# RWKV blocks of a hybrid encoder layer: one layout for both halves of the partitions, and the state's own part as small products in the chain

## The chip, the core and the metric

The kernel runs on one core of a Trainium2 chip (trn2). Its engines are TensorE (PE, matrix products, with its weight loads shown apart as PEld), VectorE (DVE), ScalarE (ACT), GpSimd (POOL) and SyncE (SP), which here issues nearly all DMA transfers. The metric is the time on the device in microseconds (us) of one execution, lower is better; the profile is of one execution.

## What is computed

One encoder layer over 2048 tokens of width 1024: a norm, one input projection, four token mixers side by side (retention, RWKV-7, a gated linear recurrence "LRU", gated linear attention "GLA", 256 columns and 4 heads of 64 each), an output projection, and 16 experts that each choose 256 tokens. The change lies in the RWKV-7 mixer, which runs a matrix state over time, once forward and once backward:

```python
def _rwkv7_direction(r, k, v, xw, xa, ...):
    ...
    def step(S, inp):
        r_t, w_t, k_t, v_t, kk_t, a_t = inp
        sa = jnp.einsum('bhvk,bhk->bhv', S, -kk_t)
        S = (S * w_t[:, :, None, :] + sa[..., None] * (kk_t * a_t)[:, :, None, :]
             + v_t[..., None] * k_t[:, :, None, :])
        return S, jnp.einsum('bhvk,bhk->bhv', S, r_t)
    ...
    _, y = lax.scan(step, jnp.zeros((B, N_GROUP_HEADS, HEAD_DIM, HEAD_DIM), r.dtype), xs)

def _rwkv7_group(...):
    y_f, b_f = _rwkv7_direction(r, k, v, ...)
    y_b, b_b = _rwkv7_direction(_flip(r), _flip(k), _flip(v), ...)
    y = y_f + _flip(y_b)
```

All inputs and outputs are fp32.

## The kernel before

The program goes through the stages projection with LRU and the RWKV inputs (`rwkv_a`), then RWKV blocks with retention and GLA beside them, then the output projection, a top-k, and the experts. In the middle stage three generators are woven (`weave`): `rwkv_rest` (the RWKV blocks, then the output weights and four early tiles of the output projection), `retention` and `gla`, in fixed shares of steps. That gives the order in which the work is written; a scheduler of the framework then places each engine's instructions, so the order on an engine differs from the written one. Each engine works through its own list in order.

RWKV works on chunks of 64 tokens, two chunks to a block of 128, 16 blocks a direction. `rwkv_b` runs rounds: in round i it prepares block i of both directions (`rwkv_prep`), runs the chain of the blocks prepared a round before (`rwkv_chain`), and loads the next blocks (`rwkv_load`); `in_turn` takes one step of each in turn. Partition halves 0 to 63 and 64 to 127 are called H[0] and H[1]; a chunk of index e uses them in an order that depends on e.

`rwkv_load` brings the block's row `bld` (640 KB), four pieces into `q1` and two into `ti`, the inverse that was computed earlier. `rwkv_prep` then makes, for four heads: p1, transposed keys (L606), which ACT moves to `q0` and `q1` with four instructions of 64 partitions (L610); p2, transposed z and v (L615), moved to `R` and `mv` (L618, L619); two banks of 64-row products (L628), masked into `R` by four DVE instructions (L633); products of keys with `rd`, a layout with zero halves that DVE copies from `bld` (L623), on PE at L639 and masked into `q0` and `q1` by four DVE instructions (L643); X = ti x R (L648), evacuated by ACT (L650); and E = q1 - X x q0 (L656, L659), a 128x128 matrix per head and chunk. `q0`, `q1` and `rd` are rings of fixed tiles, zeroed once in the halves that nothing writes; `q1` holds two identity blocks as well (`eye`).

`rwkv_chain` takes the two chunks in turn. Per chunk: four products of `E` with `mv`, one per head (L672), into one bank. One half of that bank is the new state, which DVE scales by the chunk's decay into the next chunk's `mv` (L676); the other is the output, which ACT copies to `yt` (L680), stored by SP (L683).

A bank is 512 fp32 values on each partition; the RWKV stream has four. A product in fp32 is two records in the profile, each with a weight load of its own. `tile_position` places a product on part of PE's 128x128 array.

## Time and profile before

| what | value |
|---|---|
| median of 3 runs | 2882.82 us (2876.65 to 2886.56) |
| the profiled execution, its own time | 2875.32 us |
| its span, first to last instruction | 2873.5 us |
| busy: PE / PEld / DVE / ACT / POOL | 2597.0 / 2323.1 / 1762.4 / 1381.8 / 724.3 us |
| mean granted PE clock | 0.944 of full speed |

A busy time is the time in which an instruction of that engine was running, summed without overlap. Matmuls are pipelined: a record of PE lasts longer than the distance to the next one, so the distance between starts tells the rate. "Idle before" is the time in which the engine stood just before the group's instructions, and behind the arrow stands what ended it. The granted clock is the share of full speed that the chip gave PE.

### The profile page before, as it was taken

The page shows a single profiled execution, that of the slowest core. Times are in us where ns is not written, and L with a number is a line of the kernel's source. Part 1 is how long each engine was busy: PE and PEld are TensorE (multiplying, and loading weights), DVE is VectorE, ACT ScalarE, POOL GpSimd, SP SyncE. Part 2 cuts the span into 40 slices and gives each one's busy share as a digit, 9 for nine tenths or more (in the row PEclk, how much of TensorE's full clock was granted, in tenths as well). Part 3 has the DMA queues.
Part 4 walks back from the last instruction along what each step waited for, and adds up shares of the span by engine and source line. Part 5 has one row for each costly group of instructions (what it writes and reads, how often), then busy time and mean ns, then how long its engine had stood idle before and what let it go on. Part 6 is the DMA issues. An engine that isn't in the chain of part 4 may idle for free.

```text
span 2873.5 us, 47388 instructions
## 1 busy us (share of the span) xinstructions
PE 2597.0 (90%) x18433; PEld 2323.1 (81%) x18433; DVE 1762.4 (61%) x3458; ACT 1381.8 (48%) x2302; POOL 724.3 (25%) x764
## 2 busy tenths in 40 slices
PE   6989998989878888896979659999999999999987
PEld 5866787778767777774767549999999999999987
DVE  4444567767787667888444465555555555566564
ACT  4265555435434666554533214444444444455453
POOL 0011115444524554446533310000000000000121
PEclk9999999989989989897989869999999999999999
DMA  9735554775546544445344436666666666798874
GB/s 316 268 112 184 169 167 150 215 230 167 137 115 176 171 143 147 142 135 177 109 164 142 150 97 206 206 206 206 206 206 206 206 206 206 221 294 294 264 238 142
DMA packets 474016, 538.41 MB, mean 187 GB/s; under 512 B 129952, under 2 KB 411584, under 8 KB 473024
## 3 DMA queue, kind: packets, MB, share of 16 engines
q1 hardware_dynamic: 461984, 492.12, 53.0%
q0 software_dynamic: 11808, 43.26, 5.7%
q8 instruction: 145, 2.38, 0.3%
q14 instruction: 79, 0.65, 0.1%
HBM read 392.17 MB, written 145.23 MB: 187 GB/s over the span
## 4 chain that ended last, share of the span: by engine, by line
PE 57%; DVE 14%; DMA 8%; ACT 6%; issue 4%; POOL 3%; SPq 0%; POOLq 0%; ACTq 0%; DVEq 0%
PE bank L129 46%; DMA ld<-rw_cm 3%; DMA rt_ld<-tm 1%; PE bank L639 1%; PE bank L1486 1%; DVE x L485 1%; PE bank L656 1%; DMA fn_x<-acc,x_idx 1%; PE bank L628 1%; DVE pr L484 1%; PE bank L672 1%; DVE tk_j L1389 1%; POOL pr L484 1%; PE bank L648 1%; PE bank L1467 1%
## 5 line engine op out<-in xcount | busy, mean ns | idle before, releaser
L44 DVE TENSOR_TENSOR x_wl<-x_st,x_wh 128x2048 fp32r<-128x2048 f32 x189 | 432.9, 2292 | 304.1 <-ACT x_wh L43 303.7
L129 PE MATMUL bank<-x_xh,x_wh 128*128 128x256 f32 x2048 | 580.4, 285 | 2.7 <-ACT x_wh L43 2.6
L129 PE MATMUL bank<-x_xl,x_wh 128*128 128x256 f32 x2048 | 577.8, 283 | 0.0
L129 PE MATMUL bank<-x_xh,x_wl 128*128 128x256 f32 x2048 | 572.6, 283 | 1.1 <-DVE x_wl L44 1.1
L43 ACT ACTIVATE x_wh<-x_st 128x2048 fp32r<-128x2048 f32 x192 | 367.6, 1915 | 119.6 <-PE bank L129 100.4
L129 PEld LDWEIGHTS bank<-x_xh,x_wh 128*128 128x128 f32 x2048 | 393.7, 192 | 3.5 <-ACT x_wh L43 3.0
L129 PEld LDWEIGHTS bank<-x_xl,x_wh 128*128 128x128 f32 x2048 | 393.6, 192 | 0.0
L129 PEld LDWEIGHTS bank<-x_xh,x_wl 128*128 128x128 f32 x2048 | 390.4, 192 | 1.6 <-DVE x_wl L44 1.6
L129 PE MATMUL bank<-x_wh,x_hh 128*128 128x256 f32 x1024 | 289.9, 285 | 5.7 <-ACT x_hh L43 5.7
L129 PE MATMUL bank<-x_wl,x_hh 128*128 128x256 f32 x1024 | 291.1, 285 | 0.0
L129 PE MATMUL bank<-x_wh,x_hl 128*128 128x256 f32 x1024 | 289.6, 284 | 0.0
L1612 POOL DMA_INDIRECT acc<-x_os,x_idx x30 | 48.6, 1620 | 925.3 <-ACT x_os L1546 896.7
L129 PE MATMUL bank<-h_hi,w_hi 128*128 128x512 f32 x576 | 238.3, 417 | 20.8 <-DVE o_cm L1662 13.3
L129 PE MATMUL bank<-h_lo,w_hi 128*128 128x512 f32 x576 | 239.7, 416 | 0.0
L129 PE MATMUL bank<-h_hi,w_lo 128*128 128x512 f32 x576 | 235.9, 410 | 0.0
L129 PEld LDWEIGHTS bank<-x_wh,x_hh 128*128 128x128 f32 x1024 | 196.5, 193 | 5.9 <-ACT x_hh L43 5.9
L129 PEld LDWEIGHTS bank<-x_wl,x_hh 128*128 128x128 f32 x1024 | 197.3, 193 | 0.0
L129 PEld LDWEIGHTS bank<-x_wh,x_hl 128*128 128x128 f32 x1024 | 197.1, 193 | 0.0
L129 PE MATMUL bank<-w_hi,h_hi 128*128 128x256 f32 (+1 forms) x512 | 156.5, 306 | 12.9 <-DVE o_tm L1662 9.4
L129 PEld LDWEIGHTS bank<-h_hi,w_hi 128*128 128x128 f32 x576 | 112.2, 195 | 56.8 <-DVE o_cm L1662 15.9
L129 PE MATMUL bank<-w_lo,h_hi 128*128 128x256 f32 (+1 forms) x512 | 149.0, 291 | 0.0
L129 PE MATMUL bank<-w_hi,h_lo 128*128 128x256 f32 (+1 forms) x512 | 148.4, 290 | 0.0
(448 smaller groups left out, 5520.9 us busy)
## 6 DMA issues: line engine op xcount, KB each, us to landing
x_st<-in_exp_w_gate_dram SPq DMA_DIRECT2D x64, 1024.0 KB, 8.7
x_st<-in_exp_w_up_dram SPq DMA_DIRECT2D x64, 1024.0 KB, 9.2
x_st<-in_exp_w_down_dram SPq DMA_DIRECT2D x64, 1024.0 KB, 5.3
w_st<-in_w_in_dram SPq DMA_DIRECT2D x20, 1024.0 KB, 7.6
rw_sp<-sp SPq DMA_DIRECT2D x16, 1280.0 KB, 4.6
bld<-rw_sp SPq DMA_DIRECT2D x32, 640.0 KB, 3.9
ld<-rw_cm SPq DMA_DIRECT2D x14, 899.5 KB, 6.2
cm<-o_cm SPq DMA_DIRECT2D x40, 256.0 KB, 2.8
```

Source lines behind the costliest of these rows:

```text
L43: g.nc.scalar.activation(out=hi, in_=src, func=AF.Copy)
L44: (g.nc.gpsimd if pool else g.nc.vector).tensor_tensor(out=lo, in0=src, in1=hi.bitcast(F32), op=OP.subtract)
L129: g.nc.tensor.matmul(out, lhsT=lhs[a][:, k, lsl], rhs=rhs[b][:, k, rsl], start=(k + i == 0 and out is outs[0]), stop=(3 * k + i == 3 * nk ...
L484: eng.tensor_tensor(out=pr[:, 0:i, 0:i], in0=a, in1=b, op=OP.mult)
L485: nc.vector.tensor_reduce(out=x[:, 0:i, i], in_=pr[:, 0:i, 0:i], axis=AX.X, op=OP.add)
L628: nc.tensor.matmul(pss[k][:, q * P:(q + 1) * P], lhsT=z[q][H[k]], rhs=ks, start=True, stop=True)
L639: nc.tensor.matmul(ps[:, o:o + P], lhsT=bk[q][e], rhs=rd[:, 2 * q + 1 - e], start=True, stop=True)
L648: nc.tensor.matmul(ps[:, h * P:(h + 1) * P], lhsT=ti[:, h], rhs=R[:, h], start=True, stop=True)
L656: nc.tensor.matmul(ps[:, h * 256:(h + 1) * 256], lhsT=X[:, 2 * h2 + h, :], rhs=q0[:, 2 * h2 + h].rearrange("p e c -> p (e c)"), start=True ...
L672: nc.tensor.matmul(ps[:, h, :], lhsT=E[:, h, e, :], rhs=mv[e][:, h, :], start=True, stop=True)
L1389: nc.vector.tensor_scalar(out=junk, in0=vals, scalar1=cand[:, m:m + 1], scalar2=0.0, op0=OP.is_ge, op1=OP.add, accum_out=cnt[:, m:m + 1])
L1612: g.nc.gpsimd.indirect_dma_start(out=dst, out_offset=bass.IndirectOffsetOnAxis(ap=idx[:, s:s + 1], axis=0), in_=t[:, s], in_offset=None, **kw)
```

## The change

`q0` and `q1` become one tile `Q`, [chunk, head, 128 columns], with the same layout on both partition halves: its first 64 columns come from p1 by one ACT instruction, its last 64 from the masked products by one DVE instruction. `R` is laid out alike: one ACT instruction, and two DVE ones where there were four. `rd` is no longer copied by DVE but loaded by two DMAs a block. In L628's place, 8 products of 64x64 per block on the four quarters of the array replace 4 of 64x128. `E` is built without the part that multiplies the state directly: 16 products of 64x64 weights on 128 columns replace 4 of 128x128 on 256, into two banks, one per chunk; a mask column `hm` picks the half of `Q` that is added. The part left out moves to the chain: per chunk, one product with a 64x64 identity over 256 columns and four with `rq` (the transposed keys, loaded by the four DMAs that filled `q1`, now issued in the prep) accumulate in the bank before 8 products with `E` of 128x64 weights.

```diff
@@ rwkv_b_buffers
-    g.rd = ring("rd", [P, 4, 2, C], 2, lambda t: [t[64 * k:64 * k + 64, :, 1 - k, :] for k in range(2)])
-    g.q0 = ring("q0", [P, NH, 2, P], 2, lambda t: [t[64 * e:64 * e + 64, :, 1 - e, :] for e in range(2)])
-    g.q1 = ring("q1", [P, NH, 2, P], 4, eye)
+    g.rd = ring("rd", [P, 4, 2, C], 4, lambda t: [t[64 * k:64 * k + 64, :, 1 - k, :] for k in range(2)])
...
+    g.hm = g.fp.tile([P, 2], F32, name="hm")
+    nc.vector.memset(g.hm, 1.0)
+    for e in range(2):
+        nc.vector.memset(g.hm[64 * e:64 * e + 64, e:e + 1], 0.0)
@@ rwkv_load
-    q1 = turn(g.q1)
-    for k in range(2):
-        for e in range(2):
-            s = slice(64 * e, 64 * e + 64)
-            nc.sync.dma_start(out=q1[s, k::2, e, s], in_=half[64 * k:64 * k + 64, :, 320 - 320 * e:384 - 320 * e])
...
+    rd = turn(g.rd)
+    for k in range(2):
+        s = slice(64 * k, 64 * k + 64)
+        nc.sync.dma_start(out=rd[s, :, k], in_=sp[s].rearrange("p (u t) -> p u t", t=320)[:, :, 0:C])
@@ rwkv_prep
+    Q = g.bp.tile([P, 2, NH, P], F32, name="Q", tag="Q")
...
+    rq = g.mp.tile([P, NH, C], F32, name="rq", tag="rq")
...
+    for k in range(2):
+        for e in range(2):
+            nc.sync.dma_start(out=rq[H[e], k::2], in_=half[H[k], :, 320 - 320 * e:384 - 320 * e])
...
-    for e in range(2):
-        for s, q in ((H[e], q0), (H[1 - e], q1)):
-            nc.scalar.activation(out=qh(q[s, :, e, H[1 - e]]), in_=p1[s, :, e], func=AF.Copy)
+    nc.scalar.activation(out=Q[:, :, :, 0:C], in_=p1.rearrange("p (e h c) -> p e h c", e=2, h=NH), func=AF.Copy)
...
+    nc.scalar.activation(out=R[:, :, 0:C], in_=p2[:, 0], func=AF.Copy)
     for e in range(2):
-        nc.scalar.activation(out=R[H[e], :, H[e]], in_=p2[H[e], 0], func=AF.Copy)
         nc.scalar.activation(out=mv[e][H[1 - e]], in_=p2[H[1 - e], 1], func=AF.Copy)
...
-    rd = turn(g.rd)
-    for k in range(2):
-        nc.vector.tensor_copy(out=rd[H[k], :, k], in_=ld[H[k]].rearrange("p (u t) -> p u t", t=320)[:, :, 0:C])
...
-            nc.tensor.matmul(pss[k][:, q * P:(q + 1) * P], lhsT=z[q][H[k]], rhs=ks, start=True, stop=True)
+            for e in range(2):
+                o = HALF * q + C + 3 * C * (1 - e)
+                nc.tensor.matmul(pss[k][H[e], q * C:(q + 1) * C], lhsT=z[q][H[k], H[e]], rhs=ld[H[k], o:o + C], start=True, stop=True,
+                                 tile_position=(64 * k, 64 * e))
...
+        nc.vector.tensor_tensor(out=R[:, k::2, C:P], in0=pss[k][:, 0:P].rearrange("p (q t) -> p q t", q=2),
+                                in1=c["m_bm"][:, dr, None, :].broadcast_to([P, 2, C]), op=OP.mult)
...
-        for s, q in ((H[e], q0), (H[1 - e], q1)):
-            nc.vector.tensor_tensor(out=qh(q[s, :, e, H[e]]), in0=pv[s, :, e], in1=c["m_in"][s, dr, None, None, :].broadcast_to([64, 2, 2, C]), op=OP.mult)
+    nc.vector.tensor_tensor(out=Q.rearrange("p e h c -> p (e h) c")[:, :, C:P], in0=ps.rearrange("p (n t) -> p n t", t=C),
+                            in1=c["m_in"][:, dr, None, :].broadcast_to([P, 2 * NH, C]), op=OP.mult)
...
-            nc.tensor.matmul(ps[:, h * 256:(h + 1) * 256], lhsT=X[:, 2 * h2 + h, :], rhs=q0[:, 2 * h2 + h].rearrange("p e c -> p (e c)"),
-                             start=True, stop=True)
...
+    for h in range(NH):
+        for u in range(2):
+            for e in range(2):
+                nc.tensor.matmul(pss[e][H[u], h * P:(h + 1) * P], lhsT=X[H[e], h, H[u ^ e]], rhs=Q[H[e], e, h], start=True, stop=True,
+                                 tile_position=(64 * e, 64 * u))
+    for e in range(2):
+        nc.vector.scalar_tensor_tensor(out=E[:, e].rearrange("p h c -> p (h c)"), in0=Q[:, e].rearrange("p h c -> p (h c)"), scalar=g.hm[:, e:e + 1],
+                                       in1=pss[e], op0=OP.mult, op1=OP.subtract)
@@ rwkv_chain
+        nc.tensor.matmul(ps[H[1 - e]], lhsT=g.c["eye64"][H[e]], rhs=mv[e][H[e]], start=True, stop=False, tile_position=(64 * e, 64 - 64 * e))
         for h in range(NH):
-            nc.tensor.matmul(ps[:, h, :], lhsT=E[:, h, e, :], rhs=mv[e][:, h, :], start=True, stop=True)
+            nc.tensor.matmul(ps[H[e], h, :], lhsT=rq[H[e], h, :], rhs=mv[e][H[e], h, :], start=(h == 0), stop=False, tile_position=(64 * e, 64 * e))
+        for h in range(NH):
+            for u in range(2):
+                c0 = 64 * (u ^ 1 ^ e)
+                nc.tensor.matmul(ps[c0:c0 + 64, h, :], lhsT=E[:, e, h, H[u]], rhs=mv[e][:, h, :], start=False, stop=(h == NH - 1), tile_position=(0, c0))
```

The scheduler places the instructions anew. Lines move by up to four: L606 becomes L608, L615 L614, L628 L625, L648 L642, L656 L652, L672 L670 to L676, and on DVE L633 becomes L628, L643 L636, L659 L655, L676 L680. In the rows below a product is shown by the partitions and columns of its moving operand, and `x8` is eight instructions in a row.

PE, one round late in the stretch, before: transpositions of the next blocks, one chain step of each direction (L672), and on to the second transposition.

```order
L606 MATMUL bank<-c_ident,bld 128x128 x8
L983 MATMUL bank<-c_ident,gl_y_9089 128x128 x8
L672 MATMUL bank<-mv_11481,E 128x64 x4
L672 MATMUL bank<-mv_11494,E 128x64 x4
L615 MATMUL bank<-c_ident,bld 128x128 x4
```

The same place in the changed program:

```order
L608 MATMUL bank<-c_ident,bld 128x128 x8
L670 MATMUL bank<-mv_12478,c_eye_345 64x256
L672 MATMUL bank<-mv_12478,rq 64x64 x4
L676 MATMUL bank<-mv_12478,E 64x64 x4
L1240 MATMUL bank<-gl_v,gl_sT 128x64 x4
L676 MATMUL bank<-mv_12478,E 64x64 x4
L670 MATMUL bank<-mv_12494,c_eye_345 64x256
L672 MATMUL bank<-mv_12494,rq 64x64 x4
L676 MATMUL bank<-mv_12494,E 64x64 x8
L614 MATMUL bank<-c_ident,bld 128x128 x8
```

A chain step was four products of one shape and is now thirteen of two shapes (here printed as 64x64 for `E` too, which has 128 rows of weights and 64 columns), with a GLA product (L1240) placed inside one of them.

PE, the end of a prep, before: X (L648) and then the products for `E` (L656).

```order
L648 MATMUL bank<-R,ti_7184 128x128 x4
L938 MATMUL bank<-c_ident,rt_a_9969 128x128 x4
L648 MATMUL bank<-R,ti_7185 128x128 x4
L656 MATMUL bank<-q_7166,X 128x256 x2
L952 MATMUL bank<-rt_qd_7362,rt_kT 128x256 x2
L656 MATMUL bank<-q_7167,X 128x256 x2
```

The same place in the changed program:

```order
L642 MATMUL bank<-R,ti_7172 128x128 x4
L642 MATMUL bank<-R,ti_7173 128x128 x4
L652 MATMUL bank<-Q,X 64x128 x20
L987 MATMUL bank<-c_ident,rt_y_10996 128x128 x8
L652 MATMUL bank<-Q,X 64x128 x12
```

The products for `E` of both blocks are now 32 of quarter size in two groups, parted by a transposition of retention (L987) that needs the whole array.

DVE, the masked products of one round, before (a second name q is `q1`'s tile):

```order
L643 TENSOR_TENSOR q_7166<-bank,c_m_in 64x4x64
L643 TENSOR_TENSOR q_7174<-bank,c_m_in 64x4x64
L643 TENSOR_TENSOR q_7166<-bank,c_m_in 64x4x64
L81 TENSOR_TENSOR rw_y_11844<-rw_y_11844,hn_r 128x512
L643 TENSOR_TENSOR q_7174<-bank,c_m_in 64x4x64
L643 TENSOR_TENSOR q_7167<-bank,c_m_in 64x4x64
L643 TENSOR_TENSOR q_7175<-bank,c_m_in 64x4x64
```

The same place in the changed program, up to the two subtractions that make `E`:

```order
L81 TENSOR_TENSOR rw_y_11987<-rw_y_11987,hn_r 128x512
L636 TENSOR_TENSOR Q<-bank,c_m_in 128x8x64 x2
L882 TENSOR_TENSOR rt_a_11158<-rt_ld,rt_cs 128x512
L680 TENSOR_TENSOR mv_12024<-bank,pcx 64x256
L988 SCALAR_TENSOR_TENSOR go_g<-bank,gla_gn,go_g 128x512
L680 TENSOR_TENSOR mv_12040<-bank,pcx 64x256
L1170 SCALAR_TENSOR_TENSOR gl_S_7398<-bank,gl_cc,gl_S_7398 128x64
L655 SCALAR_TENSOR_TENSOR E<-Q,hm,bank 128x512 x2
```

Eight instructions of 64 partitions in a round are now two of 128.

## Rows read from the trace of the kernel before

**Rows 1.** Windows: us, busy (count) of each engine, granted clock, DMA share, GB/s

```profile
core 0: us, PE busy (x) PEld busy (x) DVE busy (x) ACT busy (x) POOL busy (x), PEclk, DMA share, GB/s
860.00:1290.00 430.00, 376.77 (x2635) 325.21 (x2634) 322.99 (x798) 258.13 (x654) 195.76 (x296) 0.90 0.51 152
1700.00:2873.00 1173.00, 1148.36 (x9932) 1146.50 (x9931) 667.42 (x967) 558.90 (x691) 120.72 (x86) 0.99 0.69 218
```

**Rows 2.** Chain that ended last, 860 to 1290 us: shares by engine and line

```profile
by line: PE bank L639 8.1%; issue 7.2%; DMA rt_ld<-tm 6.2%; PE bank L656 6.0%; PE bank L628 5.1%; PE bank L672 4.7%; PE bank L648 3.7%; PE bank L909 2.1%; DVE q L643 2.1%; PE bank L960 2.0%; PE bank L1217 2.0%; DMA rw_y<-ysp 2.0%; PE bank L
```

**Rows 3.** Groups by line, PE, 860 to 1290 us: busy us, mean ns | idle before, releasers

```profile
L672 PE MATMUL bank<-mv,E 128*128 128x64 f32 x512 | 66.2, 279 | 4.5 <-DVE E L659 3.7 <-DVE mv L676 0.6
L656 PE MATMUL bank<-q,X 128*128 128x256 f32 x256 | 62.4, 393 | 8.8 <-ACT X L650 6.8 <-DVE q L643 1.9
L639 PE MATMUL bank<-rd,bld 128*128 128x128 f32 x241 | 43.1, 348 | 2.1 <-DVE R L633 2.1
L648 PE MATMUL bank<-R,ti 128*128 128x128 f32 x256 | 35.9, 291 | 0.8 <-PE bank L672 0.5 <-ACT X L650 0.3
L628 PE MATMUL bank<-bld 64*128 64x128 f32 x240 | 35.6, 351 | 12.8 <-DVE R L633 6.4 <-ACT yt L680 4.9 <-ACT mv L619 1.5
L615 PE MATMUL bank<-c_ident,bld 128*128 128x128 f32 x120 | 20.0, 305 | 5.9 <-ACT q L610 5.6
```

**Rows 4.** Groups by line, DVE, the same stretch

```profile
L643 DVE TENSOR_TENSOR q<-bank,c_m_in 64x256 f32<-64x256 f32 x128 | 50.6, 419 | 5.0 <-PE bank L639 3.6
L659 DVE TENSOR_TENSOR E<-q,bank 128x512 f32<-128x512 f32 x64 | 41.6, 682 | 4.9 <-PE bank L656 4.5
L633 DVE TENSOR_TENSOR R<-bank,c_m_bm 64x128 f32<-64x128 f32 x120 | 34.5, 287 | 14.8 <-PE bank L628 12.7
...
L623 DVE COPY rd<-bld 64x256 f32<-64x256 f32 x60 | 21.9, 366 | 10.8 <-DMA bld<-rw_sp 9.9
...
L984 DVE SCALAR_TENSOR_TENSOR go_g<-bank,gla_gn,go_g 128x512 f32<-128x512 f32 x3 | 2.2, 744 | 0.0
```

**Rows 5.** Groups by line, ACT, the same stretch

```profile
L610 ACT ACTIVATE q<-bank 64x256 f32<-64x256 f32 x120 | 41.3, 375 | 21.1 <-PE bank L606 19.9
...
L618 ACT ACTIVATE R<-bank 64x256 f32<-64x256 f32 x60 | 22.2, 369 | 2.2 <-PE bank L615 1.7 <-ACT xg L772 0.4
L650 ACT ACTIVATE X<-bank 128x512 f32<-128x512 f32 x32 | 18.6, 592 | 22.0 <-PE bank L648 21.7
```

**Rows 6.** Timeline of PE at the high clock: start us, length us, records

```profile
1134.80 0.72 PE L639 MATMUL bank<-rd,bld 128*128 128x128 f32 x5
1135.45 0.43 PE L1159 MATMUL bank<-gl_v,gl_kt 128*32 128x64 f32 x16
1135.82 0.94 PE L639 MATMUL bank<-rd,bld 128*128 128x128 f32 x6
1136.59 0.60 PE L952 MATMUL bank<-rt_qd,rt_kT 128*128 128x256 f32 x2
...
1186.29 1.04 PE L983 MATMUL bank<-c_ident,gl_y 128*128 128x128 f32 x8
1187.17 1.90 PE L672 MATMUL bank<-mv,E 128*128 128x64 f32 x16
```

**Rows 7.** Timeline of PE's weight loads around one group of L628 [idle before, releaser]

```profile
1167.01 1.78 PEld L628 LDWEIGHTS bank<-bld 64*128 64x128 f32 x12 [0.23 <-issue]
1169.01 3.31 PEld L639 LDWEIGHTS bank<-rd,bld 128*128 128x128 f32 x16 [0.22 <-issue]
```

**Rows 8.** DMA issues, 860 to 1290 us: count, KB each, us to landing

```profile
bld<-rw_sp SPq DMA_DIRECT2D x29, 640.0 KB, 3.9
...
ti<-rw_T SPq DMA_DIRECT2D x58, 64.0 KB, 3.4
q<-rw_sp SPq DMA_DIRECT2D x114, 32.0 KB, 2.4
```

**Rows 9.** Waits of SP's queue, the same stretch: us in total, times, longest

```profile
SPq L577 <- DVE E L659: 11.4, 7, 3.3
```

48 lines of the change are left out of this document (15 added, 33 removed).

## Prediction

> **What bounds the kernel now.** I read the windows first, to find where the change lies. The RWKV blocks (`rwkv_prep`, `rwkv_chain`) run in the 430 us from 860 to 1290, woven with the retention and GLA streams; there TensorE (PE) is busy 377 us, VectorE (DVE) 323, ScalarE (ACT) 258, and the granted PE clock is 0.90. The experts after 1700 us are PE work at 1148 of 1173 us, which the change does not touch [rows 1]. So all that can move lies in one stretch, 16 rounds of two blocks (one forward, one backward), some 27 us a round. PE stands idle only 53 us of it, but PE alone does not set the time: in the chain of work that ended last, five PE lines of the blocks take 8.1 + 6.0 + 5.1 + 4.7 + 3.7 = 27.6%, or 119 us, while one DVE line, the masked products `q` of L643, has 2.1% (9.0 us) [rows 2]. Then the groups by line. The same five PE lines are busy 243 us, so 0.49 of what PE does for the blocks is on the chain; for DVE L643 it is 9.0 of 50.6 us, 0.18 [rows 2 to 4]. Last, what PE's idle time ended on: ACT X 6.8, DVE q 1.9, DVE R 6.4, ACT yt 4.9, ACT mv 1.5, ACT q 5.6, DVE E 3.7, together 31 us on evacuations of banks [rows 3]. The reader is to see a stage in which PE has little slack, and most of that slack is waiting for DVE and ACT to empty a bank.
>
> **Evacuations, DVE and ACT.** With both halves of the partitions laid out alike, one instruction reads a bank where two or four did. An instruction of 64 partitions costs what one of 128 costs, so halving their number halves the time. For 32 blocks:
> DVE `q`: 128 x 0.419 = 53.6 becomes 32 of 128x512; that shape from a bank takes 0.682 (L659), 21.8: -31.8. DVE `R`: 128 x 0.287 becomes 64 of the same length: -18.4. DVE copies `rd`: 64 x 0.366 = 23.4, replaced by DMA: -23.4. DVE `E`: 64 x 0.682 becomes 64 scalar_tensor_tensor of the same size, 0.744 by L984: +4.0. Sum -70 us [rows 4]. ACT `q`: 128 x 0.375 = 48.0 becomes 32 of 128x512, 0.592 by L650: -29.1. ACT `R`: 64 x 0.369 becomes 32 of the same length: -11.8. Sum -41 us [rows 5]. So some 110 us of work leave the two engines. Most of it lies beside PE. I let it shorten the stage by the 0.18 found above: 20 us. The ends are nothing (another release comes last in each place) and the 37 us of the second rival below. The 0.18 is near PE's own idle 31 us times the share of evacuation work that goes, which is why I take it.
>
> **PE, the products.** Prices: on the full array a record of 128 columns comes every 0.11 us (8 of L983 in 0.88); narrow weights lie beside each other in the array: 16 records of L1159, on a quarter of the columns each, take 0.37 us in all with a change of the array's shape, four at a time [rows 6]. Take off 0.09 for the change (below): 0.07 a set.
> (a) `E`: 256 records of 256 columns, 62.4 us, become 1024 of 128 columns on the four quarters, 256 sets. A record of 128 columns averages 35.9 / 256 = 0.140 (L648), so 36 us if four run together: -26.5. Two together: 72 us, +9. No row shows quarters in rows and columns at once; L1159 shows four column strips, so I take four [rows 3, 6].
> (b) `R`'s product (L628): the columns of each record halve and quarters replace halves; 35.6 us with its own shape changes, between 0 and -17, taken as -10 [rows 3].
> (c) The chain: before, 8 records of 64 columns a step, 66.2 us for 64 steps, 1.03 each [rows 3]. After, a step has one identity product of 256 columns (2 records, 0.244 each by L656), beside it 4 products of the state's own part (8 records in a row, 8 x 0.07 = 0.56), then 8 half-width products with `E`, 8 pairs, 0.56: 1.12, or +6 us in all. From below: half of 0.11 a set, -6. From above: 0.092 a set and the identity product not beside the others but before them, 1.96, +60. I take +6, since L1159's set is the nearest row.
> (d) Changes of the array's shape. In the built program, from the first block's transposition to the last chain step, the shape changes 118 times before and 440 after, since `E`'s products are now 64x64 between 128x128 ones and each chain step goes 64x64, 128x64 and back; the scheduler also puts retention and GLA products inside the groups. Some 6 more are L628's, in (b): 316 are new. A change costs, at the high clock: 5 records of L639 before L1159 take 0.65 where 0.56 would do (+0.09), and 6 after it 0.77 where 0.67 would (+0.10), because the first weight load is exposed [rows 6]. With 64-wide loads I take 0.15: 47 us. Where the clock is low (16 weight loads of L639 in 3.31 us, 0.21 each and not 0.11) the loads stand 0.23 and 0.22 us for nothing the profile shows, at the two changes of one group of L628 [rows 7].
> PE's sum: -26.5 - 10 + 6 + 47 = +16.5 us, of which 0.49, 8 us, on the chain.
>
> **DMA and queues.** The four loads a block into `q1` (32 KB each, 2.4 us to landing) become four into `rq`, now issued in the prep and not with the load; two loads of 64 KB a block replace the `rd` copies, the size of the `ti` loads, which land in 3.4 us [rows 8]. They go out with the block's own load of 640 KB (3.9 us) and are wanted two steps after it, so that load hides them; uncovered they would cost 3.4 us in a round. What goes is SP's wait of `q1`'s loads for `E`, 11.4 us in 7 places [rows 9]; in its place `rq` waits for the chain two blocks back, a round earlier, with `ysp`, `ti` and the next block's load behind it on SP. I cost both at nothing; the 11.4 us bound either way, and only what starves PE would count.
>
> **Forecast.** -20 + 8 = -12 us on the profiled execution: 2875.3 becomes 2863. That execution lies 7.5 us under the median of 2882.8, so about 2870 as a median. The granted clock in the stretch (0.90, so about a fifth of it at 1.2 GHz and not 2.4 [rows 1]) may move either way: fewer waits, more empty moments between shapes; 8 us each way go into the range.
>
> **Rivals.**
> 1. More is gained: the rounds are bound by the string of evacuations (110 us over 16 rounds is 6.9 us of 27). For it: 31 of PE's 53 idle us end on them. Against it: PE's busy 377 + 16 us of 430 leave at most 37. Time 2846.
> 2. Nothing changes: all of PE's +16.5 lies on the path, -20 + 16.5 = -3.5 us, 2879 as a median. For it: PE is idle 12% only, and its order is fixed. Against it: five PE lines with 243 us of work have 119 on the chain.
> 3. Slower, by the shape changes: each costs what the low-clock rows show, 0.23 us, and stands on PE's in-order queue with nothing beside it. 316 x 0.23 = 73, PE +42, less 20: +22 us, 2905. It ends slower from 0.19 us a change on: 316 x 0.19 - 30.5 - 20 = +9.5. For it: "issue" has 7.2% of the chain, 31 us, with 118 changes [rows 2]. Against it: at the high clock the rows give 0.09 and 0.10. The Trainium skill (TensorEngine Tiling (Array Packing), Tiling Modes, Key Properties) says that changing the tiling mode, and not just the tile, drains the TensorE; the trace agrees, with 0.09 us at L1159, and the rule gives no price of its own.
> 4. Slower, by packing: quarters run two at a time and the identity product alone: (a) +36, (c) +31 us against the sum, PE +84, 0.49 of it less 20: +21 us, 2904. For it: L628, two halves of the rows, averages 0.148 a record, no better than L648's 0.140 on the whole array [rows 3]. Against it: L628's figure has its shape changes in it.
>
> **How the numbers follow.** About 0.3%, 8.6 us, is what a measurement of this kernel can tell from no change. Forecast 0.33, rival 1 0.14: faster 0.47. Rival 2: same 0.22. Rivals 3 and 4, 0.20 and 0.11: slower 0.31. Forecast and rival 1 with the clock's 8 us reach down to 2838; rivals 2 to 4 up to 2905, with a little for dearer changes 2908; what is left out (serial packing at the full price, or no PE slack used up at all) I hold under 0.2. The faster cases alone span 2838 to 2874.
>
> **What would show it.** In the changed profile: DVE busy in the RWKV stretch down by about 70 us and ACT by 40; a set of four `E` records every 0.11 us at the high clock; a group of 64x64 records starting about 0.2 us after the last full-array record; the waits of PE on ACT q, DVE R and DVE q gone; the stretch some 12 us shorter and everything after it only shifted. It is wrong if the stretch is longer although both engines are lighter (rival 3 or 4: look at PE's gaps at shape changes, and at starts within `E`'s sets), or if PE's new waits end on `rd`, `rq` or on the two `E` subtractions, which now free two banks at once.

## The result, and the profile after

The changed kernel takes 2897.8 us (median of 5, 2895.8 to 2903.8) against 2882.2 us before: ratio 1.0067, 95% interval 1.0052 to 1.0082. It is slower by 0.67%, where 0.4% faster was forecast. The medians lie 15.6 us apart; in the two profiled executions, from which all that follows is read, the spans are 2898.2 and 2873.5 us, 24.7 us apart.

All of that lies between the first RWKV block and the end of the output projection; what stands before and behind sums to 2084 and 2082 us. Windows of the two kernels: the whole stretch, then the RWKV phase (first to last chain step), with busy us and records of PE, PEld, DVE, ACT, POOL, then granted PE clock, DMA share, GB/s. Before:

```profile
840.60:1630.20 789.60, 679.38 (x4261) 556.87 (x4261) 518.10 (x1319) 401.49 (x948) 353.19 (x447) 0.89 0.47 148
870.20:1288.30 418.10, 367.19 (x2568) 317.25 (x2568) 312.37 (x777) 253.99 (x644) 191.60 (x290) 0.90 0.51 151
```

After:

```profile
838.50:1654.70 816.20, 705.11 (x6437) 560.25 (x6437) 463.13 (x1097) 362.97 (x816) 346.00 (x446) 0.87 0.49 149
866.10:1380.50 514.40, 454.83 (x5004) 363.39 (x5003) 294.77 (x670) 270.61 (x651) 234.29 (x342) 0.86 0.50 144
```

DVE is 55 us lighter and ACT 39, yet PE's idle time (length less PE busy) is 111.1 us and was 110.2. PE busy grew by 25.7 us. Most of that is not work: by the trace's clock records PE spent 205 us of the stretch at 1.2 GHz, before 167, and 160 of these us busy, before 123. (The time at 1.2 GHz is twice the missing share of the granted clock, times the length.) I split the stretch in three from here on: **PE work**, its busy time with the busy time at 1.2 GHz counted half; the **clock's loss**, the other half; and **idle**. The split is an estimate, as it takes work at 1.2 GHz for twice as long as at 2.4. Before 618.2 + 61.3 + 110.1; after 625.0 + 80.1 + 111.2. So of 26.6 us the clock has 18.8, PE's work 6.8, idle 1.1.

The groups of the changed lines, which answer to [rows 3 to 5], from the first block to the last chain step (838 to 1382 us; busy us, mean ns | idle before). PE:

```profile
L676 PE MATMUL bank<-mv,E 128*64 128x64 f32 x1024 | 57.9, 252 | 0.0
L672 PE MATMUL bank<-mv,rq 64*64 64x64 f32 x512 | 52.3, 247 | 0.0
L670 PE MATMUL bank<-mv,c_eye 64*64 64x256 f32 x128 | 48.2, 462 | 9.6 <-DVE E L655 6.7 <-ACT Q L609 2.8
...
L652 PE MATMUL bank<-Q,X 64*64 64x128 f32 x1024 | 44.7, 286 | 4.2 <-ACT X L644 4.2
```

DVE, in the same view (838 to 1400 us):

```profile
L655 DVE SCALAR_TENSOR_TENSOR E<-Q,hm,bank 128x512 f32<-128x512 f32 x64 | 45.0, 742 | 5.7 <-PE bank L652 5.3
...
L636 DVE TENSOR_TENSOR Q<-bank,c_m_in 128x512 f32<-128x512 f32 x32 | 21.9, 687 | 10.3 <-PE bank L635 10.3
...
L628 DVE TENSOR_TENSOR R<-bank,c_m_bm 128x128 f32<-128x128 f32 x64 | 16.9, 285 | 17.6 <-PE bank L625 17.3
```

Every price of the evacuations is the forecast one (0.742, 0.687, 0.285 us). What PE does with the time is seen in its timeline (start, us, records, idle before) around one group of quarter products, two blocks of them:

```profile
937.42 1.98 PE L652 MATMUL bank<-Q,X 64*64 64x128 f32 x64
944.55 0.69 PE L1157 MATMUL bank<-c_ident,gl_p 128*128 128x128 f32 x2 [5.15 <-POOL gl_p L1144]
```

and in windows of the same place:

```profile
937.40:944.50 7.10, 2.00 (x65) 1.74 (x64) 5.91 (x9) 3.13 (x5) 6.49 (x15) 0.98 0.65 154
944.50:968.20 23.70, 22.49 (x182) 17.42 (x182) 7.85 (x20) 9.05 (x18) 8.67 (x19) 0.50 0.42 98
```

64 quarter records take 1.98 us, so 16 sets at 0.11 with one change of shape. Then PE stands 5.15 us until POOL has made GLA's `gl_p`, which the next product on PE's list needs, and the next 23.7 us, in which PE is busy 95%, run at a granted clock of 0.50, that is at 1.2 GHz. PE's waits (from the first block to 1460 us) show where its idle time went:

```profile
PE bank L987 <- DVE rt_y L81: 22.0, 1, 22.0
PE bank L625 <- ACT mv L618: 11.6, 6, 4.3
...
PE bank L608 <- DVE E L655: 8.3, 5, 4.6
...
PE bank L670 <- DVE E L655: 6.7, 2, 3.5
```

The first is new: the RWKV blocks end at 1381 us (before 1288), the other two streams at 1403 (before 1446), and PE has nothing left beside retention's last normalisation. The second, on ACT's evacuation of `mv`, had 1.5 us before [rows 3]. The last two are the subtractions for `E`, which free two banks at once: 15.0 us of waits end on them here, 16.5 in e2 below, which has the quarters too, and 1.8 and 2.7 in e5 and e3, which have `E` on the whole array (6.0 before).

### The profile page after: what moved, and what is told of

Read it like the earlier page. It is cut to its first block, busy times and chain, and to the rows that moved or that the text cites. A ratio compares the mean times of both kernels' runs of the same rounds, so it can differ in the third digit from the quotient of the medians.

```text
span 2898.2 us, 51348 instructions
## 1 busy us (share of the span) xinstructions
PE 2619.4 (90%) x20609; PEld 2323.6 (80%) x20609; DVE 1707.3 (59%) x3237; ACT 1338.3 (46%) x2162; POOL 714.6 (25%) x764
## 5 line engine op out<-in xcount | busy, mean ns | idle before, releaser
L129 PEld LDWEIGHTS bank<-h_hi,w_hi 128*128 128x128 f32 x576 | 111.9, 195 | 56.3 <-DVE o_cm L1666 16.5
```

Source lines behind the costliest of these rows:

```text
L129: g.nc.tensor.matmul(out, lhsT=lhs[a][:, k, lsl], rhs=rhs[b][:, k, rsl], start=(k + i == 0 and out is outs[0]), stop=(3 * k + i == 3 * nk ...
```

## The experiments

All runs, with the three parts of the stretch and the us at 1.2 GHz in the RWKV phase. Ratios are to the kernel before, timed on the same chip in turn with it. The parts are those of one profiled execution each, so they need not add up to the ratio. e17 (e19 with `WR` 200) has no result.

| run | what | ratio, 95% | PE work | clock's loss | idle | low clock, RWKV |
|---|---|---|---|---|---|---|
| before | | 1 | 618 | 61 | 110 | 82 |
| after | quarters, small chain | 1.0067 [1.0052, 1.0082] | 625 | 80 | 111 | 147 |
| e1 | after, other order | 1.0082 [1.0057, 1.0107] | 610 | 80 | 131 | 116 |
| e2 | quarters, old chain | 1.0004 [0.9987, 1.0021] | 588 | 69 | 133 | 120 |
| e3 | whole array, old chain | 0.9953 [0.9934, 0.9972] | 609 | 60 | 113 | 68 |
| e5 | whole array, small chain | 0.9963 [0.9943, 0.9983] | 652 | 45 | 92 | 68 |
| e6 | after, `E` 128 wide in the chain | 1.0081 [1.0053, 1.0109] | 642 | 77 | 99 | 130 |
| e13 | halves, old chain | 1.0002 [0.9986, 1.0019] | 600 | 90 | 109 | 135 |
| e14 | halves, small chain | 0.9979 [0.9963, 0.9996] | 641 | 61 | 83 | 102 |
| e4 | before + small products, ahead of waits | 1.0014 [0.9999, 1.0029] | 663 | 42 | 91 | 44 |
| e7 | the same, behind waits | 0.9989 [0.9973, 1.0005] | 666 | 42 | 78 | 51 |
| e8 | before + whole-array products | 1.0110 [1.0093, 1.0127] | 678 | 50 | 95 | 51 |
| e9 | e2, quarters twice | 1.0137 [1.0103, 1.0170] | 614 | 84 | 132 | 139 |
| e10 | e2 + whole-array products | 1.0016 [1.0003, 1.0028] | 625 | 69 | 106 | 105 |
| e12 | e3 + small products | 1.0033 [1.0014, 1.0053] | 686 | 51 | 76 | 62 |
| e11 | after, 4 buffers for `Q` | 1.0039 [1.0018, 1.0060] | 627 | 70 | 105 | 123 |
| e15 | e3, 4 buffers for `Q` | 0.9910 [0.9877, 0.9942] | 611 | 56 | 98 | 72 |
| e18 | e5, 4 buffers for `Q` | 0.9949 [0.9933, 0.9965] | 650 | 38 | 85 | 55 |
| e16 | e3, other order | 0.9968 [0.9956, 0.9980] | 611 | 59 | 113 | 82 |
| e19 | before, three evacuations twice | 1.0309 [1.0277, 1.0341] | 623 | 110 | 154 | 188 |

**How far an order alone moves the time.** e1 and e16 change one number of the weave.

```diff
-WR, WG = 100, 68
+WR, WG = 160, 68
```

> The changed kernel with one number altered: the share of steps that the weave gives to the RWKV stream (100 becomes 160), so that the RWKV blocks end earlier and retention and GLA keep more work beside the output weights and the early output projection, as in the kernel before. In the built program 94 retention and 60 GLA products then stand behind the last chain step (14 and 8 in the changed kernel, 90 and 64 before), and the array's shape changes 332 times in the RWKV blocks instead of 440.
> Theory A, the tail: the changed kernel is slower because its RWKV stream ends last and leaves PE idle for 22 us behind the last retention normalisation with nothing left beside it. Then that wait goes, and the time falls by 15 to 28 us, to 2870 to 2883 us.
> Theory B, the shape changes: PE's 26 us of added busy time are the loss, wherever the streams end. Then only the 108 changes that the order saves count, at 0.09 to 0.15 us each: 10 to 16 us less, 2882 to 2888 us, with the idle wait replaced by another.
> Theory C, the new waits on the two subtractions for E: no change, 2893 to 2903 us.

e1 is no faster than the changed kernel. The RWKV blocks end at 1300 us, near the 1288 of before, the 22 us wait is gone, and idle time has come up elsewhere (131 us in all). Where the streams end is not the cause by itself. The same instructions with 108 shape changes fewer take 15 us less PE work, 0.14 us a change, and that does not show in the time. e16, with 130 for 100 in e3:

> The third run's kernel with the RWKV stream's share of the weave 130 instead of 100: the same instructions in a slightly other order (78 retention and 58 GLA products behind the last chain step instead of 94 and 59; 122 shape changes instead of 127). No theory expects a difference; what comes, measures how far an order alone moves the time: 0.993 to 0.998.

0.9968 beside 0.9953. Both pairs differ by 0.15%, inside their intervals, so a difference of that size between two builds says nothing here.

**The two parts of the change, one at a time.** e2 puts the state's part back into `E`: a tile `S` with the identity and the keys is what the lower or upper half of `E` is subtracted from, and the chain is the old one.

```diff
-    for e in range(2):
-        nc.vector.scalar_tensor_tensor(out=E[:, e]..., in0=Q[:, e]..., scalar=g.hm[:, e:e + 1], in1=pss[e], op0=OP.mult, op1=OP.subtract)
+    for e in range(2):
+        for s, m in ((H[1 - e], Q[:, e]), (H[e], S)):
+            nc.vector.tensor_tensor(out=E[s, e]..., in0=m[s]..., in1=pss[e][s], op=OP.subtract)
@@ rwkv_chain
+            nc.tensor.matmul(ps[:, h, :], lhsT=E[:, e, h, :], rhs=mv[e][:, h, :], start=True, stop=True)
```

> The chain's part of the change undone: the identity and the state's own part go back into E, each chain step is again four products of 128x128, and E takes four subtractions of 64 partitions where the changed kernel has two of 128; Q takes two and two evacuations of 256 columns instead of one and one of 512. The layout on both halves, the rd loads and the quarter products for E stay. 197 shape changes instead of 440.
> Theory B: 243 fewer shape changes at 0.09 to 0.15 us are 22 to 36 us of PE, and the chain's products themselves cost about what they did; DVE is 40 us heavier than in the changed kernel, of which 0.18 is on the path, +7. Time 2868 to 2883 us.
> Theory A: here the streams end in the order of the kernel before, nearly (74 retention and 44 GLA products behind the last chain step), so the idle wait is mostly gone: 2876 to 2885 us. The trace tells the two apart: by A the PE busy time of the stretch stays near 705 us and the idle time falls, by B busy falls to about 680.
> Theory C: E waits for one more subtraction on each side, so no gain, 2893 us or more.

1.0004: the chain's part is 0.63% here. The trace sides with theory B: PE's work fell by 37 us, near the 36 that 243 changes at 0.15 us make, while idle, which theory A has falling, rose by 21. e3 then takes the quarters away:

```diff
-    nc.scalar.activation(out=X, in_=ps.rearrange("p (h c) -> p h c", h=NH), func=AF.Copy)
+    nc.scalar.activation(out=X[H[0], 0], in_=pv[H[0]], func=AF.Copy)
+    for u in range(2):
+        nc.scalar.activation(out=X[H[1], 1, :, H[u]], in_=pv[H[1], :, H[1 - u]], func=AF.Copy)
...
-    for h in range(NH):
-        for u in range(2):
-            for e in range(2):
-                nc.tensor.matmul(pss[e][H[u], h * P:(h + 1) * P], lhsT=X[H[e], h, H[u ^ e]], rhs=Q[H[e], e, h], ..., tile_position=(64 * e, 64 * u))
+    for e in range(2):
+        for h in range(NH):
+            nc.tensor.matmul(pss[e][:, h * P:(h + 1) * P], lhsT=X[:, e, h], rhs=Q[:, e, h], ...)
```

> As the run before it (the state's part in E, the chain of the kernel before), and E's products too on the whole array: X is evacuated by halves beside zeros, three ACT instructions for one, and E is 8 products of 128x128 a block instead of 16 of 64x64. What is left of the change is the evacuation of Q, R and rd on all partitions at once, and R's quarter products. 127 shape changes, 118 before and 440 in the changed kernel. DVE is some 30 us lighter and ACT 18 us lighter than in the kernel before.
> Theory B: PE is where it was before, so only the lighter evacuations show: 0.18 of 48 us, 9 us under the kernel before, 2870 to 2878 us.
> Theory A: the order of the streams is that of the kernel before, so 2870 to 2885 us as well; A and B differ in the run before this one and in the order run.
> A rival to both, that the evacuations were hidden all along: 2879 to 2886 us, no change against the kernel before.

0.9953, faster than both kernels and a little below every range, with 21 us more PE work than e2. Besides the quarters, X's evacuation changes here (three ACT instructions for one), and the bank of the first chunk is full after half of the products and not at the end. e5 keeps the changed kernel's chain and takes the quarters away in the same way:

> The changed kernel with E's products on the whole array (X evacuated by halves beside zeros, 8 products of 128x128 a block) and the chain with its small products kept. Against the run with the whole array and the old chain (0.9953 of the kernel before) it adds the chain's part alone; against the changed kernel (1.0067) it takes the quarters alone away. 379 shape changes.
> The chain theory (the small products stand behind the wait for the state, so their longer step and their shape changes are paid in full, whatever E's products are): 1.001 to 1.004 of before, 2880 to 2889 us.
> The quarters theory (the changed kernel loses by E's 64x64 products, through a lower clock and through their shape changes): 0.995 to 0.999, 2862 to 2875 us.
> If both add up as measured so far (chain +0.63%, quarters +0.51%): 1.0016.

0.9963, with 379 shape changes. So the quarters, with the filling of both banks at once and the single evacuation of X that go with them, are what made the changed kernel slow: without them it is faster than before, though PE then works 27 us more. The windows of e5, the whole stretch and then the RWKV phase:

```profile
840.20:1628.80 788.60, 696.98 (x5925) 565.23 (x5925) 468.99 (x1098) 385.44 (x881) 355.12 (x447) 0.92 0.51 154
865.90:1358.60 492.70, 447.15 (x4531) 367.75 (x4532) 303.87 (x677) 292.04 (x714) 242.05 (x349) 0.93 0.53 152
```

In the RWKV phase 147 us at the low clock become 68. The two parts do not add up: the chain's small products cost 0.63% beside quarters and 0.10% beside the whole array, which is less than two builds differ by.

e6 merges two of the chain's three shapes:

```diff
-        for h in range(NH):
-            for u in range(2):
-                c0 = 64 * (u ^ 1 ^ e)
-                nc.tensor.matmul(ps[c0:c0 + 64, h, :], lhsT=E[:, e, h, H[u]], ..., tile_position=(0, c0))
+        for h in range(NH):
+            nc.tensor.matmul(ps[:, h, :], lhsT=E[:, e, h, :], rhs=mv[e][:, h, :], start=False, stop=(h == NH - 1))
```

> The changed kernel, but the chain's products with E on 128 columns at once, 8 records of the whole array a step instead of 16 of half its columns (Q takes two and two evacuations of 256 columns for that). The identity and state products stay small: one of the three shapes of a step goes, 364 shape changes instead of 440.
> The chain theory: a step of the chain took 1.30 us in the changed kernel and 1.05 before at the high clock, and one shape change of about 0.15 us of it goes, 64 steps: 10 us less than the changed kernel, 1.003 to 1.005 of before, 2885 to 2891 us.
> If it is the wait for the small products as such: no change, 1.006 to 1.008.

A miss, 1.0081: `E`'s records in the chain cost more on whole columns (83.2 us busy for 512, against 57.9 for 1024 in pairs), so PE's work rose by 17 us although 76 shape changes went. (This kernel also moves `Q` in halves, as e2 does.)

**The price of a shape change, and where it stands.** e4 puts 128 small products into the kernel before, each making a change there and back; e7 makes them wait for the same data as the products behind them.

```diff
+        nc.tensor.matmul(ps[0:64, 0:64], lhsT=c["eye64"][0:64], rhs=c["eye64"][0:64], start=True, stop=True, tile_position=(0, 0))
         for h in range(2):
             nc.tensor.matmul(ps[:, h * 256: ...
...
```

> The kernel before with one small product of 64x64 by 64 columns put ahead of each of E's 64 groups of products and of each of the chain's 64 steps; its result is overwritten by the product behind it. The array's shape changes 352 times in the RWKV blocks instead of 118; the order of the streams moves a little (62 retention and 39 GLA products behind the last chain step instead of 90 and 64).
> Theory B: 234 changes at 0.09 to 0.15 us and 128 products at about 0.06 us are 29 to 43 us of PE; all of it on the path gives 2911 to 2925 us, the share of 0.49 of the prediction 2896 to 2903 us.
> Theory A: shape changes are largely hidden by PE's slack, so under 0.3%, 2882 to 2890 us, unless the streams' end moves.
> At 0.23 us a change, the price of the low clock: +54 + 8 us of PE, 2912 (half) to 2944 us.

> The kernel before with the 128 small products of 64x64 by 64 columns of the fourth run at the same places, but reading what E's products (X) and the chain's products (the state's half of mv) wait for, so that they and both of their shape changes stand behind the wait and not ahead of it. 362 shape changes against 352.
> The theory of position: ahead of a wait the changes ran in time that PE would have idled (PE idle 110 us before, 91 there); behind it they are paid: 44 us of PE work, at least half of it on the path, 1.006 to 1.014, 2894 to 2917 us.
> The theory that PE's work has slack wherever it stands: as there, 1.000 to 1.003, 2876 to 2885 us.

PE's work rose by 44.4 us in e4: less some 8 for the products themselves (an estimate, 128 at about 0.06), that is 0.155 us for each of 234 changes, near e1's 0.14 and the forecast's 0.15. But the time rose by 0.14%, and in e7 not at all. The window of the RWKV phase in e4:

```profile
869.80:1313.40 443.60, 413.65 (x2934) 338.11 (x2934) 329.70 (x801) 269.99 (x691) 209.98 (x311) 0.95 0.50 147
```

and in e7:

```profile
871.70:1311.50 439.80, 415.40 (x2894) 340.73 (x2895) 332.17 (x805) 268.24 (x682) 206.34 (x306) 0.94 0.49 148
```

PE stands idle 30 and 24 us there (51 before) and the clock is 0.95 and 0.94 (0.90 before): the added work filled pauses, and PE's pauses of over 2 us in the phase fell from 8 to 2 and 0. Position ahead of a wait or behind it made no difference, so that theory fell. In e8 (two products of 128x128 at those places; each is two records, so 56 us of work and not the 28 that the expectation says, with `WR` 160) the clock was up too, but half of the work was paid, if the order that `WR` changes counts for as little as in e1 and e16:

> The kernel before with two useless products of 128x128 by 128 columns at the places of the small ones of the fourth run (ahead of E's products and of each chain step), so 28 us of work on the whole array without a shape change; their results are overwritten. The share of the RWKV stream in the weave is 160 instead of 100, which keeps the streams' end as in the kernel before (94 retention and 59 GLA products behind the last chain step).
> The theory of the clock (the fourth run had 45 us less at the low clock than the kernel before, 122 for 167, because PE stood empty less): the low clock falls again by 30 to 50 us and pays for most of the work: 0.997 to 1.002, 2868 to 2882 us.
> The theory of work: 28 us of PE, half or all of it on the path, 1.005 to 1.010, 2890 to 2905 us.

And in e12, the small products in e3, they were paid in part as well (1.0033 for 0.9953, 23 of 77 us; its profiled execution, 2898 us, lies above its median of 2885):

> The third run's kernel (layout on both halves, E on the whole array, old chain; 0.9953 of before) with the small products of the seventh behind the waits, 128 of 64x64 in all, whose results are overwritten. It asks whether what they did to the kernel before (48 us of PE more, 31 us less at the low clock, 0.9989) they do here too.
> Theory of the clock: low clock in the RWKV phase 68 us becomes 40 to 50, PE idle falls by some 25 us, 0.993 to 0.998.
> Theory of work: 44 us of PE, half of it on the path, 1.001 to 1.008.

So filling is no rule. What holds in all four is that of 44 to 77 us more PE work little over half shows at most, because idle time and the clock's loss shrink beside it.

**Do products on part of the array hold the clock?** e9 issues each quarter product twice, e10 puts whole-array products of about the same time there.

> The second run's kernel (state part in E, old chain, E by quarters) with every quarter product of E issued twice, the second over the first: 28 us of PE more by the measured 0.11 us a set, all of it 64x64 products at the place where they stand already. The RWKV stream's share of the weave is 130 instead of 100 so that about as much work of the other streams stands behind the last chain step (46 retention and 20 GLA products) as in the run it is paired with. That run, e10, has the same time of work on the whole array at the same place. The kernel without either was at 1.0004 of before, with 120 us at the low clock in its RWKV phase (82 before) and 9 PE pauses of over 2 us there.
> Theory: quarter products do not hold the clock up as products on the whole array do. Then the low clock stays at 110 us or more in the RWKV phase and the work is paid: 1.006 to 1.014.
> Rival: the clock falls only because the shorter quarter products leave PE idle in longer pieces; any work that fills them helps. Then low clock 50 to 90 us, and 0.998 to 1.005, as in e10.

> The second run's kernel with four useless products of 128x128 by 128 columns ahead of each block's quarter products (two records of 0.11 us each, 28 us of PE in all; their result is overwritten). 46 retention and 32 GLA products stand behind the last chain step.
> Both theories of e9: the low clock of the RWKV phase falls from 120 us to 50 to 90 and pays for much of the work, 0.998 to 1.005 of before. If instead PE's work is paid in full wherever it stands: 1.008 to 1.012, with the low clock near 120 us.

1.0137 and 1.0016, 139 and 105 us at the low clock. The times speak for it, but e10's low clock did not fall to the 50 to 90 us that both theories had, and the orders differ (idle 132 and 106 us), so e13 was made: e3 with each product of `E` on the 64 rows that hold its data instead of on 128 rows beside zeros, the same number of products in nearly the same order. Within a group the products now alternate between the two chunks, so both banks fill at the end.

```diff
-    for e in range(2):
-        for h in range(NH):
-            nc.tensor.matmul(pss[e][:, h * P:(h + 1) * P], lhsT=X[:, e, h], rhs=Q[:, e, h], start=True, stop=True)
+    for h in range(NH):
+        for e in range(2):
+            nc.tensor.matmul(pss[e][:, h * P:(h + 1) * P], lhsT=X[H[e], h], rhs=Q[H[e], e, h], start=True, stop=True, tile_position=(64 * e, 0))
```

> As the third run (state part in E, old chain, X by halves), but E's products take 64 rows by 128 columns of the array, two at a time, instead of the whole array beside zeros: the same 8 products a block, of the same columns, half the PE time (28 us less), 162 shape changes for 127. The order is nearly that of the third run (86 retention and 59 GLA products behind the last chain step; 94 and 59 there).
> F, the order: PE does not pause longer than there, so the low clock stays near 68 us in the RWKV phase; 0.991 to 0.996 of before.
> G, part of the array: low clock 100 us or more as with quarters, 0.998 to 1.003.

The window of the RWKV phase in e3:

```profile
867.70:1278.90 411.20, 360.78 (x3075) 317.41 (x3073) 293.54 (x670) 252.37 (x632) 192.68 (x295) 0.92 0.57 165
```

`E` in e3:

```profile
L659 PE MATMUL bank<-Q,X 128*128 128x128 f32 x512 | 65.1, 281 | 4.2 <-ACT X L650 4.1
```

The same two of e13, window first:

```profile
869.10:1304.20 435.10, 384.68 (x3088) 331.61 (x3087) 296.98 (x669) 254.95 (x635) 194.37 (x299) 0.84 0.54 157
```

`E` in e13:

```profile
L658 PE MATMUL bank<-Q,X 64*128 64x128 f32 x512 | 55.7, 305 | 6.8 <-ACT X L649 6.8
```

The expectation was wrong in one point: only some of the halves ran in pairs. At the high clock a record came every 0.088 us (0.114 in e3), a quarter of them within 0.03 us of the one before, so PE's work fell by 9 us and not by 28. PE is busy 0.884 of the phase in e13 and 0.877 in e3, idle 50.4 us in both, with fewer pauses of over 2 us (4 and 7), though the longest is 4.8 us and not 2.9; DVE and ACT do the same. Yet the granted clock is 0.84 against 0.92, 135 us at 1.2 GHz against 68, and the time is 0.49% longer. Other executions bear the clock out: over their whole length it is 0.936 to 0.942 in ten of e13 and 0.945 to 0.950 in five of e3. Theory F, the order of the streams, falls; that `E`'s products on half of the rows lower the clock is shown for this pair, as far as the other order inside a group and 35 more shape changes do not (234 more in e4 went with a higher clock). That the quarters do it for the same reason fits, and is not shown. e14 has the halves beside the small chain:

> The same in the kernel with the chain's small products (E by halves of the rows instead of the changed kernel's quarters; X in three evacuations). 419 shape changes; the order is nearly that of the fifth run (0.9963), the PE time of E that of the changed kernel (1.0067).
> F, the order: 0.993 to 0.998, low clock near the fifth run's 68 us.
> G, part of the array: 1.002 to 1.008, low clock 110 to 150 us, as in the changed kernel.

0.9979 and 102 us at the low clock, between whole array (0.9963, 68) and quarters (1.0067, 147). The time is in F's range and not in G's, and its interval overlaps e5's; the clock is near neither's figure, and lower than e5's on average over all executions (0.950 and 0.955). So here the halves cost clock and hardly any time.

**`Q`'s single buffer a direction, and the best version.** `bufs=4` for `Q` in the changed kernel (e11), in e3 (e15) and in e5 (e18):

```diff
-    Q = g.bp.tile([P, 2, NH, P], F32, name="Q", tag="Q")
+    Q = g.bp.tile([P, 2, NH, P], F32, name="Q", tag="Q", bufs=4)
```

> The changed kernel with four buffers for Q instead of two (one a direction), so that the next block's evacuation into Q does not wait for the subtractions that make E of the last.
> Theory C, the new waits: in the changed kernel ACT waits 13 us in Q for E's subtractions, and PE 8 us more behind it; they go, PE's 12 pauses of over 2 us become 6 or fewer, the low clock falls, 0.2 to 0.6% under the changed kernel: 1.001 to 1.005 of before.
> Otherwise (the banks that E's two subtractions free are what the next products wait for, or the waits move on): 1.005 to 1.009.

> The third run's kernel (E on the whole array, old chain, 0.9953 of before) with four buffers for Q. In the changed kernel that took 0.28% off.
> If Q's wait for E's subtractions costs here too: 0.991 to 0.994. If it cost only where the quarters get PE there early: 0.994 to 0.997.

> The fifth run's kernel (E on the whole array, the chain's small products; 0.9963 of before) with four buffers for Q, to stand beside the same with the old chain (0.9910). With two buffers the small products cost 0.1%.
> If that was their price: 0.991 to 0.993. If Q's depth helps only the old chain: 0.995 to 0.998.

In e11 1.0039 for 1.0067: ACT's 13.1 us of waiting in `Q` for `E` are gone and the time is in the range of theory C, but PE's 12 pauses of over 2 us stay. In e15 the pauses fall from 7 to 3, and with 0.9910 it is the fastest of all, 26 us under the kernel before (which was not tried with deeper buffers). Its RWKV phase:

```profile
869.00:1273.60 404.60, 360.51 (x3081) 317.85 (x3080) 294.31 (x671) 252.25 (x632) 192.43 (x298) 0.91 0.58 168
```

With the small chain the same step gives 0.9949, between the two expectations, so the small chain costs 0.4% there, with intervals that overlap a little.

**Are the evacuations on the path?** e19 doubles three of them in the kernel before (`WR` 170).

```diff
-            nc.scalar.activation(out=qh(q[s, :, e, H[1 - e]]), in_=p1[s, :, e], func=AF.Copy)
+            for _ in range(2):
+                nc.scalar.activation(out=qh(q[s, :, e, H[1 - e]]), in_=p1[s, :, e], func=AF.Copy)
```

> The kernel before with each of three evacuations issued twice (ACT q, DVE R, DVE q; the second writes the same again): 90 us more on DVE and 48 us more on ACT by the durations of the trace, nothing on PE. The RWKV stream's share of the weave is 170 instead of 100, so that 30 retention and 24 GLA products stand behind the last chain step (90 and 64 before; 14 and 8 in the changed kernel).
> The prediction's step (0.18 of this work lies on the path): 25 us more, 1.006 to 1.011.
> That they are hidden: 0.999 to 1.003, with PE idle near 110 us as before.
> That the rounds are bound by the string of evacuations: two thirds or more of it shows, 1.03 or more.

```profile
840.60:1727.30 886.70, 733.15 (x4261) 594.29 (x4261) 607.94 (x1575) 441.95 (x1074) 351.23 (x447) 0.84 0.42 132
```

The window of the whole stretch: DVE and ACT are busy 90 and 40 us more, and the stretch is 97 us longer: idle +43, and the clock's loss +49 (277 us at 1.2 GHz for 167). The last expectation holds: added evacuations are on the path, for 0.75 of their time, and here the clock costs as much as the pauses do. `WR` differs as well, which by e1 and e16 is worth far less.

## Why the prediction was wrong

**What bounds the kernel** was read right in part. That PE has little slack and that its slack ends on evacuations holds [rows 3]; that PE's own work therefore sets half of the time does not hold as a rule (e4, e7: 44 and 48 us more for +0.14% and -0.11%; e8: 60 us more, and half of it shows).

**The sum.** For the stretch of the two profiled executions the forecast had -20 us for evacuations, +8 for PE and nothing for the clock, -12 in all. Measured are +1 us of idle time, +7 of PE's work and +19 of the clock's loss, +27 in all. So PE's term came out, and two did not: the 20 us did not arrive, and the clock took 19.

**Evacuations.** Prices and sums were right (the changed lines of DVE -69 us, of ACT -41, by count and mean). Their worth, 0.18 on the path, was read off one DVE line and used for all, and no run measures it by itself. e3, with the lighter evacuations and without quarters in `E`, is 0.5% faster than before, and e5, with 34 us more PE work than before, 0.4%. Added, the same work costs far more than 0.18 (e19). But in the changed kernel none of it arrived: idle stayed at 111 us. Of the waits named in [rows 3] most became smaller or went, as said, but that on `mv` grew from 1.5 to 11.6 us, and those on `E` (15 us, which the last lines of the forecast name as a sign) and retention's tail (22 us) came.

**PE.** Quarters run four at a time, 0.11 us a set (rival 4 falls, and (a) holds as PE work); a change costs 0.155 us (0.15 taken; rival 3's 0.23 falls). (b), -10 us, holds too (L625 25.8 us busy for all its records, L628 35.6 for 240 of 256 [rows 3]). The chain's step went from 1.06 to 1.30 us, first start to last end, at the high clock where no other stream's product stands inside it: 15 us for 64 steps, where (c) has 6, but with shape changes in it that (d) counts. In most steps another stream's product does stand inside (26 of 47 at the high clock, 7 of 59 before). PE's work in sum rose by 6.8 us, 16.5 were forecast. The lower bound of (c) is worked out wrong (16 records at 0.055 are 0.88 us a step, -10 and not -6), and the 37 us given to the second rival stand in the first; neither changes the forecast.

**The step that failed** is what (a) was taken to be worth: 26.5 us less PE work, 0.49 of it as time gained, with the clock free to move by 8 us either way. e5 and the changed kernel measure it. With quarters PE's work is 27 us less, as (a) has it; but PE stands 20 us longer and the low clock takes 35 us more, and the kernel is 1.04% slower, some 30 us. Against the kernel before the clock took 18.8 us in the profiled pair; over all executions its mean is 0.942 (5) for 0.946 (104), which is at most some 12 of the 15.6 us between the medians. The argument there was about shapes and empty moments between them, and those turned out to be harmless (e4, e7: 234 changes more, and a higher clock). That the replaced products use part of the array, and that PE is done with them so early that it stands in pieces of up to 5 us behind them, was not costed. The Trainium skill (TensorEngine Tiling (Array Packing), Performance Considerations, PSUM Bottleneck) says that tiling speeds up TensorE but not the evacuation of PSUM; the trace agrees as to the waits that end on `E`'s subtractions, 15.0 us with quarters and 1.8 in e5, while the longest pause, 5.15 us, ended on GLA's `gl_p`.

**Everything after only shifted** was wrong for the tail: the RWKV stream ended 92 us later and the others earlier. No run shows that it costs time: e1 ends its streams in the old order and is no faster, e5 has a wait of 20.9 us at the same place and is faster than the kernel before.

**Rivals.** The time, 2898, lies between rival 2's 2879 and the 2904 and 2905 of rivals 4 and 3, but by none of their mechanisms; that it lies in the stated range is luck, as rivals with other causes set that end. Rival 1's string of evacuations binds when work is added to it (e19), but taking 110 us off did not shorten the rounds. What remains open: why the small chain costs 0.6% beside quarters and 0.1 to 0.4% beside the whole array, and beside halves gains 0.2%, of which 0.15 may be nothing; and how much of the quarters' low clock comes from the pauses and how much from the part of the array in use, since only for halves the two were held apart.

## What to carry to other kernels

Before making a matmul smaller in a stage where PE waits for other engines, ask what PE does with the time: here 27 us of saved PE work came back as 20 us of idle time and 35 us of the clock's loss (e5 against after). Count idle pieces and us at the low clock beside busy time in every comparison, since a stage with equal busy share can run at 0.84 or 0.92. Test a change of layout and a change of product shape apart: the layout, with `R`'s quarter products, was worth 0.3 to 0.5% (0.9% with more buffers), and the shapes of `E` and of the chain took it away.

## What the runs showed of the hardware

- Products of `E` on half of the array's rows, in nearly the same order and at the same busy share: granted clock 0.84 and not 0.92 over 435 and 411 us (e13, e3).
- A change of the array's shape costs about 0.155 us of PE time (e4: 234 of them, 36 us; e1: 108 fewer, 15 us), yet 234 more left the time within 0.2%.
- At the high clock 64x64 products of 128 columns run four at a time, 0.11 us a set; 64x128 products that alternate between the two halves of the rows come 0.088 us apart, a quarter of them within 0.03 us of the one before, and 128x128 ones 0.114.
- PE stayed at 1.2 GHz for 23.7 us while it was busy 95% of them, behind a pause of 5.15 us (the changed kernel, from 944.5 us on).
